# The output projection of a hybrid decoder block as seven Strassen products

## The chip, the cores and the metric

The kernel runs on one core of a Trainium2 chip. Its time is the device time in microseconds of one execution, as the median of three runs; the profile is of one further execution. Engines are named as the profile names them: PE is TensorE's matmuls, PEld its weight loads, DVE VectorE, ACT ScalarE, POOL GpSimd, SP SyncE, which only issues transfers here.

## The reference

One decoder block on 512 tokens of 1024 features in float32. Two mixers, retention and windowed attention, are projected, gated and merged; the merged features go through the output projection `w_out` (1024 x 1024), a norm and a residual; then a squared-ReLU MLP of 4096 features.

```python
merged = jax.nn.sigmoid(gate_r) * y_r + jax.nn.sigmoid(gate_s) * y_s
x = x + rmsnorm(merged @ w_out[l], post_mix_norm[l])
h = rmsnorm(x, pre_mlp_norm[l])
u = jnp.square(jax.nn.relu(h @ w_up[l]))
x = x + rmsnorm(u @ w_down[l], post_mlp_norm[l])
```

The change touches the second line, and how the third gets its input.

## The kernel before, in words

Every matmul on float32 data is done as three (`mm3`, L170 to L175): each operand is split into a rounded high part, which ScalarE writes (`split`, L129), and a low part, the rest, which VectorE writes (L130); then high x high, high x low and low x high are summed in a PSUM bank. So whatever is multiplied costs an instruction of ScalarE and one of VectorE first. `parts` does this for weights, into tiles `whi` and `wlo` of 128 x 1024 with four buffers each; `moving_parts` does it for a weight tile of 128 x 2048 in two halves. Raw weights arrive in `raw`, which has two buffers.

Most projections are already done in seven products of half-size blocks instead of eight (`wide` for the retention's values and its gate, `wino_pair` for the mixers' gates and the up projection). Sums of weight blocks that these need are partly made by transfers: a plain one brings a block (SP's queue), and one issued by POOL adds a second block onto it in SBUF.

The output projection is not among them. The merged features stand transposed in `sgr`, features on partitions, tokens along. The gates' last products end with sgr's last two blocks: `ret_proj` multiplies the retention's output (bank `yr`), VectorE scales it (L882) and adds the attention's part (L883). Each of the eight blocks is split into `mhi`, `mlo`. `w_out` comes in four pieces of 1 MB, split into `wo` (`load_wo`). Then, for tokens 0 to 255 and then 256 to 511, four banks `ps` take 24 matmuls of 512 columns each: 192 in all.

After each half follows the norm chain, marked to go ahead of other work (CHAIN_AHEAD): ScalarE squares each bank with a running sum (L951), VectorE weighs it with the gain (L976) and forms the mean (L952, L121), POOL takes the reciprocal root (`rstd`, L122), VectorE adds the residual into `x1` (L977), ScalarE squares that (L951), and after the same few steps VectorE writes h2 (L981, into `zg`). TensorE transposes h2 (L1029, bank `tin`, 16 of 128 x 128 for each half of the tokens), ScalarE and VectorE split it into `h2c` for the first half and `h2b`, `h2d` for the second, and the first three pairs of up blocks (`first_ups`, bank `up`, 24 matmuls of 256 columns each) run on it while the sums for the Strassen part of the up projection are made (`wino_tokens`).

The tile framework orders each engine's instructions from the program's order and the given priorities; within an engine they start in that order.

Of the kernel before, what the change touches and what calls it, by code (L numbers as in the profile page):

```python
# [10 lines left out]
F32 = mybir.dt.float32  # L11
F32R = mybir.dt.float32r
# [4 lines left out]
P = 128  # L17
D_MODEL = 1024
SEQ = 512
# [75 lines left out]
def block_kernel(ctx, tc, x, xT, pre_mix, w_in, w_v, w_g, w_gate, w_ret, w_swa, w_out, sinks, post_mix,  # L95
                 pre_mlp, w_up, w_down, post_mlp, decay, chunk, dist, out):
    nc = tc.nc
    x, out = x[0], out[0]
    w_in, w_ret, w_swa, w_out = (w[0] for w in (w_in, w_ret, w_swa, w_out))
# [6 lines left out]
    def bank(shape, name="ps"):  # L106
        return psum.tile(shape, F32, tag="ps", name=name)
# [19 lines left out]
    def split(hi, lo, src):  # L127

        last["hi"] = nc.scalar.copy(hi, src)  # L129
        last["split"] = nc.vector.tensor_tensor(lo, src, f(hi), op=ALU.subtract)  # L130

    def raw_tile(shape):
        return stream.tile(shape, F32, name="raw", tag="raw", bufs=2)
# [30 lines left out]
    def moving_parts(raw):  # L164
        nr, width = raw.shape[1], raw.shape[2]
        h = nr // 2
        tiles = [parts(raw[:, i * h : (i + 1) * h, :], [P, h, width]) for i in range(2)]
        return [(tiles[k // h][0][:, k % h, :], tiles[k // h][1][:, k % h, :]) for k in range(nr)]

    def mm3(ps, a, b, first, last, more=False):  # L170

        (ah, al), (bh, bl) = a, b
        nc.tensor.matmul(ps, ah, bh, start=first, stop=False, skip_group_check=more)  # L173
        nc.tensor.matmul(ps, ah, bl, start=False, stop=False, skip_group_check=more)  # L174
        nc.tensor.matmul(ps, al, bh, start=False, stop=last, skip_group_check=more)  # L175

# [695 lines left out]
    def ret_proj(bp, wr):  # L872

        for b in range(2):
            fb = 2 * bp + b
            ps = bank([P, SEQ], "yr")
            for k in range(KD):
                mm3(
                    ps, tuple(a[:, k, :] for a in wr[b]),
                    tuple(a[:, k, :] for a in retT), k == 0, k == KD - 1,  # L880
                )
            nc.vector.tensor_tensor(sig[fb], ps, sig[fb], op=ALU.mult)  # L882
            nc.vector.tensor_add(sig[fb], sig[fb], ys[fb])  # L883
# [11 lines left out]
    hctx.close()  # L895


    wctx = ExitStack()
    wpool = wctx.enter_context(tc.tile_pool(name="wpool", bufs=1))
    mctx = ExitStack()  # L900
    mpool = mctx.enter_context(tc.tile_pool(name="mpool", bufs=16))
    fctx = ExitStack()
    wo = []

    def load_wo(n, pool):
        wo.append([pool.tile([P, KD, 512], F32R, name=f"wo{i}{n}") for i in range(2)])
        for kq in range(2):
            raw = raw_tile([P, 4, 512])
            nc.sync.dma_start(
                raw,  # L910
                w_out[kq * 512 : (kq + 1) * 512, n * 512 : (n + 1) * 512].rearrange(
                    "(k p) c -> p k c", p=P
                ),
            )
            for k2 in range(2):
                sl = slice(kq * 4 + k2 * 2, kq * 4 + k2 * 2 + 2)
                split(wo[n][0][:, sl, :], wo[n][1][:, sl, :], raw[:, k2 * 2 : k2 * 2 + 2, :])

    merged = []
    for bp in range(KD // 2):  # L920
        if bp == KD // 2 - 1:
            ret_proj(bp, wr)
            load_wo(0, wpool)
        for b in range(2):
            hi = mpool.tile([P, SEQ], F32R, name="mhi", tag="m")
            lo = mpool.tile([P, SEQ], F32R, name="mlo", tag="m")
            split(hi, lo, sig[2 * bp + b])
            merged.append((hi, lo))
# [8 lines left out]
    tmp = tctx.enter_context(tc.tile_pool(name="tmp", bufs=3, side="right"))  # L937
    fpool = fctx.enter_context(tc.tile_pool(name="fpool", bufs=1))
    load_wo(1, fpool)
# [3 lines left out]
    nc.sync.dma_start(g_mlp, pre_mlp.to_broadcast([P, D_MODEL]))  # L943
    for t in range(NT):
        nc.sync.dma_start(x1[t], x[t * P : (t + 1) * P, :])

    def square_sum(srcs, junk):
        ss = small.tile([P, 2], F32, name="ss2")
        for i, s in enumerate(srcs):
            c = slice(i * 512, (i + 1) * 512)  # L950
            nc.scalar.activation(junk[:, c], s, AF.Square, accum_out=ss[:, i : i + 1])  # L951
        nc.vector.tensor_add(ss[:, 0:1], ss[:, 0:1], ss[:, 1:2])  # L952
        return rstd_of(ss[:, 0:1], 1, 1.0 / D_MODEL)

    h2 = []
    for half in range(2):
        zs = [[None, None], [None, None]]
        for n in range(2):
            for t in range(2):
                tt = 2 * half + t  # L960
                ps = bank([P, 512])
                for k in range(KD):
                    mm3(
                        ps, tuple(a[:, tt * P : (tt + 1) * P] for a in merged[k]),
                        tuple(a[:, k, :] for a in wo[n]), k == 0, k == KD - 1,
                    )
                zs[t][n] = ps
        with tc.high_priority(offset=CHAIN_AHEAD):
            for t in range(2):
                tt = 2 * half + t  # L970
                hn = tmp.tile([P, D_MODEL], F32, name="zg")
                r = square_sum(zs[t], hn)
                zg = tmp.tile([P, D_MODEL], F32, name="zg")
                for n in range(2):
                    c = slice(n * 512, (n + 1) * 512)
                    nc.vector.tensor_tensor(zg[:, c], zs[t][n], g_post[:, c], op=ALU.mult)  # L976
                nc.vector.scalar_tensor_tensor(  # L977
                    x1[tt], zg, r[:, 0:1], x1[tt], op0=ALU.mult, op1=ALU.add
                )
                r = square_sum([x1[tt][:, :512], x1[tt][:, 512:]], hn)  # L980
                nc.vector.scalar_tensor_tensor(hn, x1[tt], r[:, 0:1], g_mlp, op0=ALU.mult, op1=ALU.mult)  # L981
                h2.append(hn)

    NH = 3
    fctx.close()
    mctx.close()
    wctx.close()
# [355 lines left out]
```

## Time and profile before

| | |
|---|---|
| three runs | 730.77, 731.11, 731.98 us; median 731.11 |
| the profiled execution | 731.96 us |
| its span | 730.2 us |
| granted TensorE clock, mean | 0.997 |
| PE busy | 718.1 us, 98% of the span |
| DVE, ACT, POOL busy | 535.6, 423.8, 60.5 us |
| output projection, first matmul | at 356.2 us of the span |
| first transposes of h2 | at 394.55 us |
| second transposes of h2 | at 410.27 us |

A row of a window gives its length, then for each engine the busy time and the number of instructions, then the granted clock, the mean busy share of the transfer engines and their rate. A row of the timeline gives start, duration, engine, line, operation, what is written and read; in brackets the idle time before it and what ended that. Successive instructions overlap in the records: what one costs its engine is the distance between starts, not the duration.

### The profile page before, as it was taken

What the parts mean: (1) busy time and instruction counts of PE and PEld (TensorE: products, weight loads), DVE (VectorE), ACT (ScalarE), POOL (GpSimd) and SP (SyncE); (2) the same over time, 40 slices, a digit from 0 to 9 for tenths busy, and PEclk for the clock granted to TensorE, in tenths of its full rate; (3) what the DMA queues carried; (4) which work ended last, traced back from release to release, by engine and by line L of the source; (5) the groups of instructions that cost most, each with busy time, mean ns of one, the idle gap of its engine ahead of it and who ended that gap; (6) DMA issues with size and microseconds to landing.
All of it is one profiled execution on the core that took longest, in us unless ns stands there. A gap on an engine that the chain in (4) does not pass through costs nothing.

```text
span 730.2 us, 11250 instructions
## 1 busy us (share of the span) xinstructions
PE 718.1 (98%) x4438; PEld 640.3 (88%) x4438; DVE 535.6 (73%) x808; ACT 423.8 (58%) x714; POOL 60.5 (8%) x75
## 2 busy tenths in 40 slices
PE   8999999999999999999999999999999999999996
PEld 8877878888888999989888999999999888888885
DVE  5699976677975756566944866677676788987797
ACT  6667676445665534435634865766667756555571
POOL 0200000211100000000011101100000010010010
PEclk9999999999999999999999999999999999999998
DMA  9954434907444446543661619766753899698603
GB/s 314 331 170 85 104 83 144 289 4 145 87 144 117 143 117 179 151 133 115 216 247 58 160 49 283 198 172 169 197 147 117 266 291 238 156 203 200 116 0 116
DMA packets 43749, 117.79 MB, mean 161 GB/s; under 512 B 3504, under 2 KB 21296, under 8 KB 37552
## 3 DMA queue, kind: packets, MB, share of 16 engines
q1 hardware_dynamic: 36928, 80.76, 31.5%
q0 software_dynamic: 6480, 36.18, 26.4%
q8 instruction: 35, 0.57, 0.3%
q10 hardware_dynamic: 288, 0.14, 0.1%
q14 instruction: 18, 0.15, 0.1%
HBM read 114.96 MB, written 2.10 MB: 160 GB/s over the span
## 4 chain that ended last, share of the span: by engine, by line
PE 67%; DVE 5%; DMA 2%; issue 1%; ACT 1%; POOL 1%; POOLq 0%; DVEq 0%; ACTq 0%
PE wino L173 10%; PE wino L174 10%; PE wino L175 10%; PE p L174 5%; PE p L173 5%; PE p L175 5%; PE yr L173 2%; PE yr L174 2%; PE ps L174 2%; PE yr L175 2%; PE ps L175 2%; PE ps L173 2%; DVE wlo L130 2%; PE up L175 2%; PE up L174 2%; PE up L173 2%
## 5 line engine op out<-in xcount | busy, mean ns | idle before, releaser
L130 DVE TENSOR_TENSOR wlo<-raw,whi 128x1024 fp32r<-128x1024 f32 x81 | 98.6, 1222 | 49.6 <-ACT whi L129 49.6
L129 ACT CAST whi<-raw 128x1024 fp32r<-128x1024 f32 x81 | 84.7, 1051 | 41.4 <-DMA raw<-in_w_down 7.5
L174 PE MATMUL p<-wlo,left 128*128 128x512 f32 x216 | 84.2, 390 | 0.0
L175 PE MATMUL p<-whi,left 128*128 128x512 f32 x216 | 84.1, 390 | 0.0
L173 PE MATMUL p<-whi,left 128*128 128x512 f32 x216 | 84.0, 390 | 0.1
L175 PEld LDWEIGHTS p<-whi,left 128*128 128x128 f32 x216 | 40.5, 188 | 9.1 <-DVE left L130 0.8
L174 PEld LDWEIGHTS p<-wlo,left 128*128 128x128 f32 x216 | 40.6, 188 | 8.7 <-DVE wlo L130 0.3
L173 PEld LDWEIGHTS p<-whi,left 128*128 128x128 f32 x216 | 40.5, 188 | 8.8 <-ACT left L129 0.5
L130 DVE TENSOR_TENSOR wlo<-tch,whi 128x1024 fp32r<-128x1024 f32 x32 | 38.6, 1219 | 7.5 <-ACT whi L129 7.5
L129 ACT CAST left<-uc 128x1024 fp32r<-128x1024 f32 x28 | 29.3, 1052 | 23.2 <-PE p L174 23.2
L130 DVE TENSOR_TENSOR left<-uc,left 128x1024 fp32r<-128x1024 f32 x28 | 34.1, 1220 | 10.2 <-ACT left L129 10.2
L129 ACT CAST p<-rs 128x1024 fp32r<-128x1024 f32 x21 | 22.0, 1050 | 31.2 <-DVE rs L224 31.2
L129 ACT CAST whi<-tch 128x1024 fp32r<-128x1024 f32 x32 | 33.2, 1050 | 11.7 <-PE p L175 6.8
L130 DVE TENSOR_TENSOR p<-rs,p 128x1024 fp32r<-128x1024 f32 x21 | 25.7, 1225 | 14.7 <-ACT p L129 14.7
L130 DVE TENSOR_TENSOR wlo<-rs,whi 128x1024 fp32r<-128x1024 f32 x21 | 25.7, 1224 | 10.5 <-ACT whi L129 8.4
L173 PE MATMUL wino<-h2c,whi 128*128 128x256 f32 x104 | 29.4, 283 | 0.0
L174 PE MATMUL wino<-h2c,whi 128*128 128x256 f32 x104 | 29.4, 283 | 0.0
L175 PE MATMUL wino<-h2c,wlo 128*128 128x256 f32 x104 | 29.4, 283 | 0.0
L174 PE MATMUL wino<-h2s,p 128*128 128x256 f32 x104 | 29.4, 283 | 0.0
L175 PE MATMUL wino<-h2s,p 128*128 128x256 f32 x104 | 29.4, 283 | 0.0
L173 PE MATMUL wino<-h2s,whi 128*128 128x256 f32 x104 | 29.4, 283 | 0.0
L174 PE MATMUL wino<-h2s,whi 128*128 128x256 f32 x104 | 29.4, 283 | 0.0
(350 smaller groups left out, 2328.7 us busy)
## 6 DMA issues: line engine op xcount, KB each, us to landing
tch<-in_w_down POOLq DMA_DIRECT2D x12, 1024.0 KB, 9.6
raw<-in_w_down SPq DMA_DIRECT2D x7, 1024.0 KB, 7.6
rs<-in_w_up SPq DMA_DIRECT2D x13, 512.0 KB, 4.1
rs<-in_w_up POOLq DMA_DIRECT2D x13, 512.0 KB, 5.4
raw<-in_w_up SPq DMA_DIRECT2D x13, 512.0 KB, 5.1
raw<-in_w_in SPq DMA_DIRECT2D x8, 512.0 KB, 5.3
acc<-in_w_v POOLq DMA_DIRECT2D x4, 1024.0 KB, 8.0
rs<-in_w_gate SPq DMA_DIRECT2D x8, 512.0 KB, 3.7
```

What stands on the lines that cost most here:

```text
L129: last["hi"] = nc.scalar.copy(hi, src)
L130: last["split"] = nc.vector.tensor_tensor(lo, src, f(hi), op=ALU.subtract)
L173: nc.tensor.matmul(ps, ah, bh, start=first, stop=False, skip_group_check=more)
L174: nc.tensor.matmul(ps, ah, bl, start=False, stop=False, skip_group_check=more)
L175: nc.tensor.matmul(ps, al, bh, start=False, stop=last, skip_group_check=more)
```

## The change

With the four blocks of the merged features (token half, feature half) m11, m12, m21, m22 and the four blocks of the weights, the projection becomes seven products of 24 matmuls each, into two banks for the two blocks of 128 tokens. `w_out` is laid out beforehand in blocks of 512 x 512, so that one plain transfer brings a block. The sums of weight blocks `ta` and `tb2` are made by one plain and one or two adding transfers; `b22` is used once as it came, then block (1,0) is added onto it by a transfer and it is used again; `tb2` is used once, then VectorE adds `b21` onto it (L1048 of the changed file) and it is used again. The sums of the merged features are made in place by VectorE (L952, L1024, L1025, L1036). Results leave the banks through copies on ScalarE and sums on VectorE into SBUF (L1021, L1043, L1055), and for tokens 0 to 255 the squares and the weighing (L994) read them there. The norm chain then runs for two blocks of tokens at once (L1000 the residual, L1010 h2). The first transposes of h2 are told to stand behind the last matmul of the products. The shared scratch for `zg` gets a fourth buffer. The core of the diff:

```diff
+    tb2 = weight_sum("tb2")
+    n22, n11, a12 = merge_parts("n22"), merge_parts("n11"), merge_parts("a12")
+    ta = weight_sum("ta")
+    b22 = weight_sum("b22")
+    s1, s4, s2 = (merge_parts(n) for n in ("s1", "s4", "s2"))
+    copies = [opool.tile([P, 2, 512], F32, name=f"copy{i}") for i in range(3)]
...
+    def t_load(dst, *blocks):
+        for n, (i, j) in enumerate(blocks):
+            if n:
+                nc.gpsimd.dma_start(dst, w_out[i, j], accum_op=ALU.add)
+            else:
+                nc.sync.dma_start(dst, w_out[i, j])
...
+    w11 = moving_parts(wide_load(w_out, 0, 0))
+    b21 = wide_load(w_out, 0, 1)
+    t_load(ta, (0, 0), (1, 0))
+    t_load(b22, (1, 1))
+    t_load(tb2, (0, 0), (1, 0), (1, 1))
+    split_scaled(n11[0], n11[1], m11, -1.0)
+    ret_proj(KD // 2 - 1, wr)
+    split(a12[0], a12[1], m12)
+    w21 = moving_parts(b21)
+    nc.vector.tensor_tensor(m21, m21, m22, op=ALU.subtract)
+    split(s1[0], s1[1], m21)
...
+    product(chain, n11, w11)
+    for tb in range(2):
+        nc.scalar.copy(copies[0][:, tb], chain[tb])
+    product(p2, a12, w21)
+    for tb in range(2):
+        nc.vector.tensor_tensor(zcols(tb, 0), p2[tb], copies[0][:, tb], op=ALU.subtract)
+        weighed(tb, 0)
+    nc.vector.tensor_tensor(m11, m11, m21, op=ALU.subtract)
+    nc.vector.tensor_tensor(m12, m12, m11, op=ALU.subtract)
+    product(p35, s1, moving_parts(ta))
+    split(s4[0], s4[1], m12)
...
+    w = moving_parts(b22)
+    nc.gpsimd.dma_start(b22, w_out[1, 0], accum_op=ALU.add)
+    product(p35, s4, w, False)
+    split(s2[0], s2[1], m11)
+    split_scaled(n22[0], n22[1], m22, -1.0)
+    nc.vector.tensor_tensor(m22, m22, m11, op=ALU.subtract)
...
+        w = moving_parts(tb2)
+    product(chain, s2, w, False)
+    with tc.high_priority(offset=CHAIN_AHEAD):
+        for tb in range(2):
+            nc.scalar.copy(copies[2][:, tb], chain[tb])
+            ins = nc.vector.tensor_tensor(zcols(tb, 1), p35[tb], copies[2][:, tb], op=ALU.add)
+            weighed(tb, 1)
...
+        nc.vector.tensor_tensor(tb2, tb2, b21, op=ALU.add)
+    s3 = merge_parts("s3", "n11")
+    split(s3[0], s3[1], m22)
+    product(chain, s3, moving_parts(b22), False)
+    with tc.high_priority(offset=CHAIN_AHEAD):
+        for tb in range(2):
+            z = copies[1][:, tb]
+            nc.vector.tensor_tensor(z, chain[tb], z, op=ALU.add)
+        normed((0, 1))
...
+    product(chain, n22, moving_parts(tb2), False)
+    with tc.high_priority(offset=CHAIN_AHEAD):
...
+        normed((2, 3))
...
-    with tc.high_priority(offset=H2_AHEAD):
+    with tc.issue_after(last["mm"].ins), tc.high_priority(offset=H2_AHEAD):
         transpose_h2(0)
```

In the order of instructions three places show what moves. First VectorE from the last block of the merged features on. Before (`mlo`: low halves of the merged features, `wo`: of w_out):

```order
L882 TENSOR_TENSOR sgr_2343<-yr_3577,sgr_2343 128x512
L130 TENSOR_TENSOR wo11_3644<-raw_3645,wo01_3643 128x1024
L883 TENSOR_TENSOR sgr_2343<-sgr_2343,ys_2150 128x512
L130 TENSOR_TENSOR wo11_3644<-raw_3645,wo01_3643 128x1024
L130 TENSOR_TENSOR mlo_3623<-sgr_2343,mhi_3622 128x512
L130 TENSOR_TENSOR wo11_3644<-raw_3651,wo01_3643 128x1024 x2
L976 TENSOR_TENSOR zg_3774<-ps_3665,g_post_3657 128x512
```

And now (`wlo_3622` is a half of w21, `wlo_3721` and `wlo_3725` are those of `ta`, `a12` and `s1` low halves of operands):

```order
L882 TENSOR_TENSOR sgr_2343<-yr_3588,sgr_2343 128x512
L883 TENSOR_TENSOR sgr_2343<-sgr_2343,ys_2150 128x512
L130 TENSOR_TENSOR wlo_3622<-raw_3551,whi_3621 128x1024
L952 TENSOR_TENSOR sgr_2343<-sgr_2343 128x4x256
L130 TENSOR_TENSOR a121_3529<-sgr_2343,a120_3528 128x1024
L1024 TENSOR_TENSOR sgr_2343<-sgr_2343 128x4x256
L130 TENSOR_TENSOR s11_3533<-sgr_2343,s10_3532 128x1024
L1025 TENSOR_TENSOR sgr_2343<-sgr_2343 128x4x256
L1021 TENSOR_TENSOR zg_3704<-p2_3652,copy0_3538 128x512
L130 TENSOR_TENSOR wlo_3721<-ta_3530,whi_3720 128x1024
L994 TENSOR_TENSOR zg_3704<-zg_3704,g_post_3642 128x512
L130 TENSOR_TENSOR wlo_3725<-ta_3530,whi_3724 128x1024
```

Where four splits and then the norm stood, there now stand sums and splits of operands and of weight sums, the first results between them.

Second, VectorE ahead of h2 of the first tokens. Before, with `wlo` halves of the up weights:

```order
L952 TENSOR_TENSOR ss2_3766<-ss2_3766 128x1
L976 TENSOR_TENSOR zg_3774<-ps_3715,g_post_3657 128x512
L121 TENSOR_SCALAR ms_3770<-ss2_3766 128x1
L977 SCALAR_TENSOR_TENSOR x1_3632<-zg_3774,rstd_3771,x1_3632 128x1024
L130 TENSOR_TENSOR wlo_4022<-raw_4019,whi_4021 128x1024
L130 TENSOR_TENSOR wlo_4026<-raw_4019,whi_4025 128x1024
L952 TENSOR_TENSOR ss2_3778<-ss2_3778 128x1
L976 TENSOR_TENSOR zg_3796<-ps_3690,g_post_3657 128x512
```

And now, from the second use of `b22` on (`wlo_3842`, `wlo_3846`; `wlo_3918` is of `tb2` after its last sum):

```order
L130 TENSOR_TENSOR s31_3838<-sgr_2343,s30_3837 128x1024
L130 TENSOR_TENSOR wlo_3842<-b22_3531,whi_3841 128x1024
L130 TENSOR_TENSOR wlo_3846<-b22_3531,whi_3845 128x1024
L1043 TENSOR_TENSOR zg_3704<-p35_3718,copy2_3540 128x512
L1048 TENSOR_TENSOR tb2_3523<-tb2_3523,raw_3551 128x2048
L994 TENSOR_TENSOR zg_3704<-zg_3704,g_post_3642 128x512
L1043 TENSOR_TENSOR zg_3710<-p35_3719,copy2_3540 128x512
L988 TENSOR_TENSOR ss2_3706<-ss2_3706 128x1
L130 TENSOR_TENSOR wlo_3918<-tb2_3523,whi_3917 128x1024
L1055 TENSOR_TENSOR copy1_3539<-chain_3650,copy1_3539 128x512
L994 TENSOR_TENSOR zg_3710<-zg_3710,g_post_3642 128x512
L121 TENSOR_SCALAR ms_3876<-ss2_3706 128x1
```

The norm of the first tokens now stands behind and between the weight halves of the last two products, whose sources are sums.

Third, TensorE at the first transposes of h2. Before:

```order
L174 MATMUL ps_3859<-wo11_3644,mhi_3622 128x512
L175 MATMUL ps_3859<-wo01_3643,mlo_3623 128x512
L173 MATMUL ps_3884<-wo01_3643,mhi_3526 128x512
L1029 MATMUL tin_3987<-ident_67,zg_3765 128x128
L1029 MATMUL tin_3987<-ident_67,zg_3787 128x128
```

And now:

```order
L173 MATMUL chain_3651<-whi_3921,n220_3524 128x512
L174 MATMUL chain_3651<-wlo_3922,n220_3524 128x512
L175 MATMUL chain_3651<-whi_3921,n221_3525 128x512
L1113 MATMUL tin_4019<-ident_67,zg_3886 128x128
L1113 MATMUL tin_4027<-ident_67,zg_3886 128x128
L1113 MATMUL tin_4035<-ident_67,zg_3886 128x128
L1113 MATMUL tin_4043<-ident_67,zg_3886 128x128
L1113 MATMUL tin_4019<-ident_67,zg_3896 128x128
```

They stood at the start of the last bank's 24 matmuls, with 23 behind them; now all 168 are ahead of them, and four need only the first 128 tokens' h2. The second sixteen stand behind 73 up matmuls before, behind 61 (four of them) and 67 (twelve) now. On POOL the adding transfers of `ta`, `tb2` (two) and `b22` stand ahead of the first reciprocal root.

More of the change, by code (lines that the diff above doesn't have):

```diff
@@ L174, in mm3 @@
         nc.tensor.matmul(ps, ah, bl, start=False, stop=False, skip_group_check=more)
-        nc.tensor.matmul(ps, al, bh, start=False, stop=last, skip_group_check=more)
+        return nc.tensor.matmul(ps, al, bh, start=False, stop=last, skip_group_check=more)
     def wino_pool(stack, side="left"):
@@ L919, in block_kernel, with weight_sum @@
[L919 to L928, printed above, removed]
+    octx = ExitStack()
+    opool = octx.enter_context(tc.tile_pool(name="opool", bufs=1))
+    def weight_sum(name):
+        return opool.tile([P, 4, 512], F32, name=name)
@@ new lines, in block_kernel, with merged, product @@
+    ta = weight_sum("ta")
+    b22 = weight_sum("b22")
+    s1, s4, s2 = (merge_parts(n) for n in ("s1", "s4", "s2"))
+    copies = [opool.tile([P, 2, 512], F32, name=f"copy{i}") for i in range(3)]
+    def merged(i, j):
+        return sgr[:, 2 * j : 2 * j + 2].rearrange("p m (b h) c -> p m b h c", h=2)[:, :, :, i]
+    m11, m12, m21, m22 = (merged(i, j) for i in range(2) for j in range(2))
+    def product(ps, a, w, first=True):
+        for tb in range(2):
+            for k in range(4):
+                last["mm"] = mm3(
+                    ps[tb], tuple(o[:, k // 2, k % 2, tb * P : (tb + 1) * P] for o in a), w[k],
+                    first and k == 0, k == 3, not first,
+                )
@@ L929, in block_kernel, with two @@
+    def two(name):
+        return [bank([P, 512], name) for _ in range(2)]
+    w11 = moving_parts(wide_load(w_out, 0, 0))
[9 more added lines that the diff above has]
+    split(s1[0], s1[1], m21)
     actx.close()
@@ L942, in block_kernel @@
     nc.sync.dma_start(g_post, post_mix.to_broadcast([P, D_MODEL]))
-    nc.sync.dma_start(g_mlp, pre_mlp.to_broadcast([P, D_MODEL]))
     for t in range(NT):
         nc.sync.dma_start(x1[t], x[t * P : (t + 1) * P, :])
[L947 to L951, printed above, removed]
+    nc.sync.dma_start(g_mlp, pre_mlp.to_broadcast([P, D_MODEL]))
@@ L952, in square_sum, with sum_rstd @@
+    def sum_rstd(ss):
         nc.vector.tensor_add(ss[:, 0:1], ss[:, 0:1], ss[:, 1:2])
         return rstd_of(ss[:, 0:1], 1, 1.0 / D_MODEL)
[L955 to L982, printed above, removed]
@@ new lines, in block_kernel @@
+    with tc.issue_after(after.ins):
+        nc.vector.tensor_tensor(tb2, tb2, b21, op=ALU.add)
[3 more added lines that the diff above has]
+    with tc.high_priority(offset=CHAIN_AHEAD):
+        for tb in range(2):
+            z = copies[1][:, tb]
+            nc.vector.tensor_tensor(z, chain[tb], z, op=ALU.add)
+        normed((0, 1))
+        for tb in range(2):
+            z = copies[1][:, tb]
+            c = part(2 + tb, 1, z)
+            nc.vector.tensor_tensor(zcols(2 + tb, 1), z, g_post[:, c], op=ALU.mult)
```

83 lines of the change are left out of this document (57 added, 26 removed).

## The prediction

> **What bounds the kernel now.** I read the page's shares and chain first, then the stage around the output projection in windows.
>
> ```profile
> PE 718.1 (98%) x4438; PEld 640.3 (88%) x4438; DVE 535.6 (73%) x808; ACT 423.8 (58%) x714; POOL 60.5 (8%) x75
> PE 67%; DVE 5%; DMA 2%; issue 1%; ACT 1%; POOL 1%; POOLq 0%; DVEq 0%; ACTq 0%
> core 0: us, PE busy (x) PEld busy (x) DVE busy (x) ACT busy (x) POOL busy (x), PEclk, DMA share, GB/s
> 345.00:356.20 11.20, 11.20 (x53) 9.34 (x52) 10.53 (x14) 8.62 (x14) 0.00 (x0) 1.00 0.47 158
> 356.20:367.00 10.80, 10.80 (x49) 8.93 (x48) 7.89 (x10) 5.21 (x7) 0.00 (x0) 1.00 0.92 338
> 367.00:378.00 11.00, 11.00 (x51) 9.09 (x50) 3.84 (x6) 4.21 (x9) 0.57 (x1) 1.00 0.58 241
> 378.00:389.00 11.00, 11.00 (x50) 9.13 (x49) 7.94 (x14) 4.64 (x12) 3.56 (x3) 1.00 0.52 192
> 389.00:402.00 13.00, 13.00 (x70) 11.06 (x69) 6.06 (x12) 6.13 (x16) 0.55 (x1) 1.00 0.00 1
> 402.00:413.00 11.00, 10.98 (x94) 10.77 (x93) 9.03 (x14) 8.47 (x20) 3.42 (x5) 1.00 0.81 192
> ...
> 424.00:438.00 14.00, 14.00 (x119) 14.00 (x118) 7.06 (x7) 9.04 (x16) 0.00 (x0) 1.00 0.20 63
> ```
>
> TensorE fills every window: from 356.2 (call it T0, the first output-projection matmul) on, this stage is bound by TensorE alone. VectorE is busy 7.89 + 3.84 + 7.94 + 6.06 = 25.7 of 45.8 us up to 402: it has some 20 us to spare there, no more.
>
> ```profile
> 356.20:394.30 38.10, 38.07 (x168) 31.53 (x168) 2.73 (x4) 3.38 (x10) 1.00 0.58 221
> 394.55 1.91 PE L1029 MATMUL tin<-ident,zg 128*128 128x128 f32 x16
> 401.40:410.30 8.90, 8.78 (x73) 8.79 (x73) 0.75 (x2) 1.00 0.68 176
> 410.27 2.13 PE L1029 MATMUL tin<-ident,zg 128*128 128x128 f32 x16
> 412.15 0.36 PE L174 MATMUL up<-h2c,whi 128*128 128x256 f32 x1
> ```
>
> The first row is of the projection's bank alone, the third of the up projection's: 168 matmuls of 512 columns take 38.1 us (0.227 each), 73 of 256 columns 8.75 (0.12). Transposes stand between, unwaited for; the second sixteen are over at 412.15 = T0 + 55.95, with 73 up matmuls done.
>
> **TensorE's part.** Seven products of 24 matmuls replace 192: 168, over at T0 + 38.1 if nothing is late. 24 x 0.227 = 5.45 us go. But all 16 first transposes now stand behind the 168, where they had 23 projection matmuls behind them as cover. They need h2 of tokens 0 to 255, so the question is when VectorE has it.
>
> **VectorE's part.** Counted by form, it gets 17 more instructions of 1024 elements (splits of seven weight sums and seven operand sums, the sums themselves), one of 2048, and two fewer of 512. Their prices:
>
> ```profile
> 349.31 1.22 DVE L130 TENSOR_TENSOR wo<-raw,wo 128x1024 fp32r<-128x1024 f32 x1
> 350.44 0.68 DVE L130 TENSOR_TENSOR mlo<-sgr,mhi 128x512 fp32r<-128x512 f32 x1
> 351.04 0.69 DVE L882 TENSOR_TENSOR sgr<-yr,sgr 128x512 f32<-128x512 f32 x1
> 344.14 0.69 DVE L281 TENSOR_TENSOR sgs<-sgs,wino 128x512 f32<-128x512 f32 x1 [1.46 <-PE wino L175]
> 402.61 1.29 DVE L981 SCALAR_TENSOR_TENSOR zg<-x,rstd,g_mlp 128x1024 f32<-128x1024 f32 x1 [0.73 <-POOL rstd L122]
> 403.81 0.15 DVE L952 TENSOR_TENSOR ss<-ss 128x1 f32<-128x1 f32 x1
> 408.24 0.15 DVE L121 TENSOR_SCALAR ms<-ss 128x1 f32<-128x1 f32 x1
> 408.54 0.56 POOL L122 TENSOR_TENSOR rstd<-ms,mhalf 128x1 f32<-128x1 f32 x1 [0.65 <-DVE ms L121]
> 409.14 1.28 DVE L981 SCALAR_TENSOR_TENSOR zg<-x,rstd,g_mlp 128x1024 f32<-128x1024 f32 x1 [0.74 <-POOL rstd L122]
> ```
>
> From start to start: 1.14 for 1024 elements, 0.60 for 512 (from PSUM too; rows of 256 as in L281 cost no more), 1.20 for the norm's 1024, some 0.1 for the smallest. The one of 2048 has no row: 2.2 (two of 1024) to 2.4 (two durations); I take 2.2, since starts, not ends, follow each other. Net 17 x 1.14 + 2.2 - 1.2 = 20.4 us: what was spare is gone. So I walk its queue from T0 in the new order, where the last mixer block's product (L882) is ready at 0.2.
>
> (a) To the low half of `b22`, 17 rows: 2 x 0.6 and 0.1 for their dependence, six of 1.14 (one weight half, three sums, two operand splits), then 4 x 0.6 and 5 x 1.14: ends at 16.5. Every input is there by then: the second product's first bank, for L1021, at 5.45 + 2.7 = 8.2 against 8.4.
>
> (b) Only now may the transfer that adds block (1,0) onto `b22` start.
>
> ```profile
> acc<-in_w_g POOLq DMA_DIRECT2D x4, 1024.0 KB, 8.0
> 171.76 8.02 DMA acc<-in_w_g
> 179.80 1.06 ACT whi L129
> 180.88 1.23 DVE L130 TENSOR_TENSOR wlo<-acc,whi 128x1024 fp32r<-128x1024 f32 x1 [2.27 <-ACT whi L129]
> tch<-in_w_down POOLq DMA_DIRECT2D x12, 1024.0 KB, 9.6
> DMA to landing us min/median/max: 6.1/8.0/12.7
> raw<-in_w_out SPq DMA_DIRECT2D x4, 1024.0 KB, 5.1
> ```
>
> The retention's gate does the same thing already: an adding transfer of 1 MB lands 8.0 us after its issue, ScalarE rounds, VectorE subtracts. Nothing else is moving at T0 + 17 (the 2.5 MB of x and gains, which lie in 356.2 to 367, are through), so I take 8.0, not the 9.6 of the crowded stage nor the 6.1 that the shortest of `acc`, plain ones included, shows: issue 16.6, landing 24.6, ScalarE's cast to 25.7. VectorE, with six more rows of 1.14, is free at 23.3 and waits 2.4. ScalarE's queue stands behind that cast too: the copies and squares of tokens 0 to 255 follow it.
>
> (c) From 25.8: two low halves (28.1), then in VectorE's order eight of 0.6, 2.2 for `tb2`, three weight halves, three norm operations of 1.20 and 0.8 of small ones = 4.8 + 2.2 + 3.4 + 3.6 + 0.8 = 14.8. h2 of the first 128 tokens is there at **42.9**, of the next at **44.1**. TensorE meets this twice: the seventh product, due at 32.7, needs the low halves of `tb2`, which by the same walk begin at 32.2 and 34.7, so it stands some 1.5 us and ends near 39.7; then it stands 3.1 us until 42.9, does four transposes, stands until 44.1, does twelve (1.25 us).
>
> (d) The second half: 1.4 (two products with the gain, small sums), four low halves of h2 with small ones 2.6, two norm operations 2.4, three low halves of up weights 3.4 and 0.3 small: 54.2; two norm operations: 55.4 and 56.6; twelve transposes: **57.95**, with 67 up matmuls done. The second pair's weights wait in this queue as well, so up matmuls stand some 2.5 us for them.
>
> Against before: 57.95 - 55.95 = 2.0 us later, and 73 - 67 = 6 matmuls of 0.12 still owed: **+2.7 us**. The rest is equal: up matmuls and, behind them, the next stage; VectorE makes up its lag while they run (it was idle 7 of the 14 us after 424).
>
> The other transfers I cost at nothing. `ta` and `tb2` can load only when the last gate product has read hsum, 12 matmuls of 0.12 after L281's 344.14, near 345.6; plain megabytes landed in 5.1, so `ta`'s sum is complete near T0 + 2 (used at 5) and `tb2`'s two additions, 8 each, near 16 (used at 17.5, and ScalarE has 2 us to spare behind it). POOL issues `b22`'s after them, in turn. If that cover goes, it is (b) again, us for us. The reciprocal root on POOL stood 0.15 + 0.56 behind VectorE and is hidden in (c) by the rows between.
>
> **The clock.** TensorE stands 3.1 us at one place, as nowhere since the start.
>
> ```profile
> 1.37 3.36 PE L330 MATMUL warm<-ident 128*128 128x128 f32 x14 [1.37 <-POOL ident masks.py:199]
> 722.74 0.28 PE L175 MATMUL p4c<-whi,left 128*128 128x256 f32 x1
> 725.00:726.00 1.00, 0.00 (x0) 0.00 (x0) 0.50 (x1) 0.00 (x0) 0.47 (x1) 0.74 0.00 0
> 726.00:728.00 2.00, 0.00 (x0) 0.00 (x0) 1.05 (x3) 0.00 (x0) 0.00 (x0) 0.50 0.44 159
> ```
>
> After the last matmul the granted clock fell to half within 2.5 us, so here it should fall too. At the start 14 pieces took 0.24 each, twice the 0.12 of the sixteen transposes. If half speed lasts 3.4 us (about the warm-up's length) from the first transposes, it covers those and a few up matmuls, most of which would wait for VectorE anyway: +0.3. If it lasts through the first 24 up matmuls (2.9 us more), ScalarE's first Relu comes that much later, and the squares of tokens 256 to 511 stand behind it; less a slack of 1 us: +1.9. Below zero it can't go. I take 0.3. The Trainium skill, "TensorE: Matmul & The Clock Gate" (Part 1), says half rate follows an idle window of about 3.4 us and ends after a busy one of as much, the windows running freely; by that a wait of 3.1 holds none, and the sum would be +2.7. The trace's end, with 2.5 us, speaks for a shorter wait being enough, and I follow it.
>
> Sum: +3.0. The profiled execution took 731.96 around its span of 730.2, 0.85 above the median of 731.11; 731.96 + 3.0 = 735.0, as a median **734.1**.
>
> **Rivals.** (1) *The clock stays half through the first up block*: +2.7 + 1.9 = 4.6, so 735.7. For it the fall at 725; against it that the first up matmuls stand close. (2) *The addition onto `b22` lands early*: at 22.2, when ScalarE comes free of the last operand split. VectorE then begins (c) at 23.4 instead of 25.8: +2.7 - 2.4 = +0.3, 731.4, no measurable change. Against it the 8.02 above. The Trainium skill, "DMA: Bandwidth & Descriptors" ("Anatomy of one DMA — SWDGE (gpsimd) path"), fits 2.0 us + bytes / 436e3, an estimate of 4.4 us for 1 MB; by it the sum would be this rival's; the adding transfers of this trace take nearly twice that. (3) *The saving stays*: TensorE never stands, 731.1 - 5.45 = 725.7. h2 would have to be there at 38.1, 4.8 us before my walk; rival 2 gives 2.4 of it, the rest would need VectorE's rows some 5% shorter than any row shows. It decides once the walk to h2 ends before T0 + 40 or so.
>
> **Numbers.** Forecast 0.63, (1) 0.17, (2) 0.13, (3) 0.07. A change under 0.2% (1.5 us) can't be told from none here: slower 0.80, same 0.13, faster 0.07. The forecast's own range is 732.8 to 735.0: VectorE's starts 2% either way over 57 us. The whole range goes from rival 2 (731.3) to rival 1 with the transfer at 9.6 instead of 8.0 (735.7 + 1.6 = 737.3).
>
> **What would show it.** TensorE idle about 1.5 us in the seventh product and 3 before the first transposes of h2, both released by VectorE; 2 to 3 us more before up matmuls; VectorE nearly full from 357 to 410 but for one wait of about 2.4 for the second use of `b22`, ended by an adding transfer of 8 us; a granted clock under 1 near 400. I am wrong if the transposes follow the 168 at once, or if a weight sum is late in the first four products.

## The result, and the profile after

The changed kernel takes 742.27 us (median of four runs, 741.82 to 743.03) against 731.30 for the kernel before (four runs, 730.77 to 731.98): ratio 1.0148, 95% interval 1.0136 to 1.0160. It is slower by 11.0 us, where 3.0 was forecast; 742.27 lies above the whole range that the prediction gave (731.3 to 737.3). The profiled execution took 743.03 around a span of 741.2. The page's shares and chain:

```profile
PE 721.0 (97%) x4414; PEld 642.5 (87%) x4414; DVE 554.7 (75%) x824; ACT 435.4 (59%) x725; POOL 65.1 (9%) x79
PE 37%; DVE 4%; issue 1%; DMA 1%; ACT 1%; POOL 0%; POOLq 0%; DVEq 0%; ACTq 0%
```

The shares hardly differ from those of before; the loss sits in one stage. Its windows, with the columns and bounds of the prediction's table:

```profile
356.20:367.00 10.80, 10.80 (x49) 8.93 (x49) 9.98 (x10) 7.33 (x9) 0.87 (x1) 1.00 1.02 261
367.00:378.00 11.00, 7.76 (x23) 5.85 (x22) 7.76 (x9) 5.34 (x9) 1.58 (x2) 0.69 1.04 330
378.00:389.00 11.00, 10.63 (x47) 8.44 (x46) 7.01 (x7) 6.09 (x7) 0.18 (x1) 1.00 0.68 141
389.00:402.00 13.00, 12.87 (x56) 9.86 (x54) 12.54 (x17) 9.13 (x21) 3.09 (x2) 1.00 0.24 81
402.00:413.00 11.00, 7.10 (x46) 6.56 (x46) 10.23 (x21) 8.17 (x19) 4.37 (x6) 0.84 0.51 139
413.00:424.00 11.00, 9.37 (x67) 9.38 (x68) 9.59 (x14) 6.96 (x19) 1.99 (x2) 0.84 0.75 244
```

TensorE is no longer full: 23 matmuls where there were 51 (367 to 378), 46 where there were 94 (402 to 413). In the first two windows the transfer engines are full (share 1.02 and 1.04, before 0.92 and 0.58). VectorE is idle for 3.2 and 4.0 us in the second and third, where the walk had one wait of 2.4. The waits view of VectorE from 357 to 406, in us in total, times, longest:

```profile
DVE wlo L130 <- ACT whi L129: 3.9, 1, 3.9
DVE zg L994 <- DMA g_post<-in_post_mix_norm: 3.8, 1, 3.8
DVE sgr L882 <- PE yr L175: 2.9, 1, 2.9
DVE x L1000 <- POOL rstd L122: 0.5, 1, 0.5
DVE zg L1010 <- POOL rstd L122: 0.4, 1, 0.4
```

The third row lies before the first product. The first is `tb2`: ScalarE rounds it only when its sum has come. The transfers, from issue to landing (last column), the adding ones on POOL's queue:

```profile
tb<-in_w_out POOLq DMA_DIRECT2D x2, 1024.0 KB, 12.2
ta<-in_w_out SPq DMA_DIRECT2D x1, 1024.0 KB, 5.0
ta<-in_w_out POOLq DMA_DIRECT2D x1, 1024.0 KB, 12.8
b<-in_w_out POOLq DMA_DIRECT2D x1, 1024.0 KB, 9.1
g_post<-in_post_mix_norm SPq DMA_DIRECT2D x1, 512.0 KB, 13.7
```

Each addition was forecast at 8.0, and the gain `g_post`, 6.3 before, was not in the sum at all. What TensorE meets, with two rows of VectorE and one of POOL:

```profile
372.12 0.79 PE L174 MATMUL p<-wlo,s 128*128 128x512 f32 x1 [3.24 <-DVE wlo L130]
405.68 3.62 PE L1113 MATMUL tin<-ident,zg 128*128 128x128 f32 x16 [3.81 <-ACT whi L129]
390.51 2.28 DVE L1048 TENSOR_TENSOR tb<-tb,raw 128x2048 f32<-128x2048 f32 x1
392.71 0.68 DVE L994 TENSOR_TENSOR zg<-zg,g_post 128x512 f32<-128x512 f32 x1
396.55 1.55 POOL L122 TENSOR_TENSOR rstd<-ms,mhalf 128x1 f32<-128x1 f32 x1 [18.37 <-DVE ss L988]
```

The first transposes start at 405.68, 49.4 us behind the first product (T0 = 356.25); the walk said 42.9. The profile names a cast of ScalarE as what ended TensorE's wait. But h2 is what sets it: in each of the fourteen kernels that were run with the change the first transposes start 1.43 or 1.44 us behind the start of VectorE's first row of h2 (404.25 here), whatever is named. The row of 2048 elements takes 2.20 from start to start, as assumed. POOL's root takes 1.55, not the 0.56 of the prediction's row. In the kernel before it had both lengths already: 1.55 and 1.46 (at 383.02) beside VectorE rows with two inputs in SBUF, 0.55 to 0.57 where VectorE stood or its row read a bank:

```profile
379.35 1.55 POOL L122 TENSOR_TENSOR rstd<-ms,mhalf 128x1 f32<-128x1 f32 x1 [4.40 <-DVE ms L121]
```

### The profile page after: what moved, and what is told of

Its sections match the earlier page's. It is cut to its first block, busy times and chain, and to the rows that moved or that the text cites. A ratio compares the mean times of both kernels' runs of the same rounds, so it can differ in the third digit from the quotient of the medians.

```text
span 741.2 us, 11260 instructions
## 1 busy us (share of the span) xinstructions
PE 721.0 (97%) x4414; PEld 642.5 (87%) x4414; DVE 554.7 (75%) x824; ACT 435.4 (59%) x725; POOL 65.1 (9%) x79
## 5 line engine op out<-in xcount | busy, mean ns | idle before, releaser
L130 DVE TENSOR_TENSOR wlo<-raw,whi 128x1024 fp32r<-128x1024 f32 x85 | 103.5, 1222 | 49.9 <-ACT whi L129 49.7
L129 ACT CAST whi<-raw 128x1024 fp32r<-128x1024 f32 x85 | 89.1, 1052 | 45.2 <-PE yr L174 8.1
L175 PEld LDWEIGHTS p<-whi,left 128*128 128x128 f32 x216 | 40.5, 188 | 9.1 <-DVE left L130 0.8
L174 PEld LDWEIGHTS p<-wlo,left 128*128 128x128 f32 x216 | 40.5, 188 | 8.9 <-DVE wlo L130 0.4
L173 PEld LDWEIGHTS p<-whi,left 128*128 128x128 f32 x216 | 40.5, 188 | 8.7 <-ACT left L129 0.5
```

What stands on the lines that cost most here:

```text
L175: return nc.tensor.matmul(ps, al, bh, start=False, stop=last, skip_group_check=more)
```

## The experiments

Three theories. **A**: VectorE's queue sets h2, every wait in it moves h2 by as much, and the unforecast waits come from transfers that crowd each other. **B**: VectorE's longer queue alone. **C**: the halved TensorE clock. All edits are to the changed kernel.

**e1, `tb2` summed by VectorE.**

```diff
-    t_load(tb2, (0, 0), (1, 0), (1, 1))
...
+    nc.vector.tensor_tensor(tb2, ta, b22, op=ALU.add)
     nc.gpsimd.dma_start(b22, w_out[1, 0], accum_op=ALU.add)
```

> VectorE makes the sum of tb2 from ta and b22 (one row of 128x2048, 2.2 us) and tb2's three transfers, 3 MB, are gone. Theory A (the adding transfers crowd the queues: g_post's gain comes 14 us after its issue, tb2's sum lands at 381.8, and the walk of VectorE's queue gives the rest): g_post and ta land 4 to 6 us earlier, the third product runs without its wait of 3.6 us, the fifth product is no more held until 384; 735 to 738. Theory B (VectorE's longer queue alone is the loss): 2.2 us more of VectorE ahead of h2, so 744.5. Theory C (the half clock after the wait in the third product is most of the loss): as A if that wait goes, with clock 1.0 from 371 to 378.

Measured 746.25 (ratio 1.0199, interval 1.0184 to 1.0214): slower than the changed kernel, a miss for A, and slower than B's number too. VectorE's timeline shows why:

```profile
360.93 2.29 DVE L1031 TENSOR_TENSOR tb<-ta,b 128x2048 f32<-128x2048 f32 x1 [8.18 <-DMA ta<-in_w_out]
```

The sum was put first in VectorE's queue, which then stood until `ta`'s addition landed at 360.9, with the last mixer block's product queued behind it. The edit made a wait of its own: it doesn't settle the matter.

**e2, `tb2` summed by GpSimd.** The sum takes the place of the three transfers, on POOL.

```diff
-    t_load(tb2, (0, 0), (1, 0), (1, 1))
+    nc.gpsimd.tensor_tensor(tb2, ta, b22, op=ALU.add)
```

> The same sum of tb2 from ta and b22, made by GpSimd instead of VectorE; tb2's three transfers are gone. A: as with the sum on VectorE but 2 us less of VectorE's queue, if GpSimd needs under 10 us for 128x2048: 734 to 736. B: VectorE's rows are the same as in the changed kernel, so 742. C: as A.

Measured 742.18 (1.0143, 1.0128 to 1.0158): B's number again. Its timeline, one row of POOL and two of VectorE:

```profile
360.77 5.13 POOL L947 TENSOR_TENSOR tb<-ta,b 128x2048 f32<-128x2048 f32 x1 [9.93 <-DMA ta<-in_w_out]
361.33 5.66 DVE L130 TENSOR_TENSOR s<-sgr,s 128x1024 fp32r<-128x1024 f32 x1
366.91 1.21 DVE L1025 TENSOR_TENSOR sgr<-sgr 128x1024 f32<-128x1024 f32 x1
```

A VectorE row of 1.14 took 5.58 from start to start: it began beside POOL's addition and was over about 1 us behind the end of that. The waits for `g_post` and `tb2` are gone. In their place came 4.44 us of standing inside an instruction, which no waits view lists, and a wait of 2.85 for `b22`'s addition. The Trainium skill, "SBUF — State Buffer" ("Who interferes with whom"), says that a VectorE instruction with two SBUF inputs contends with a GpSimd one that reads SBUF, and that this contention is an exclusive lock; this row agrees.

**e4, `g_post` first.** It is loaded ahead of the stage's weights.

```diff
+    g_post = opool.tile([P, D_MODEL], F32, name="g_post")
+    nc.sync.dma_start(g_post, post_mix.to_broadcast([P, D_MODEL]))
...
-        junk = opool.tile([P, 512], F32, name="junk")
+        junk = copies[0][:, t % 2]
```

To make room, the squares' unused output goes into `copies[0]`; e3 and e10 have the same.

> Only the gain g_post is loaded earlier, ahead of the weights of this stage; all adding transfers stay. A: the wait of 3.8 us at the weighing and the half clock from 371 to 378 go, but tb2's second addition still lands near 382, and the fifth product waits for that: 741 to 742.5, no gain to speak of. B: 742. C: the half clock of 6.8 us and the wait of 3.6 us in the third product go, so 736 to 738.

Measured 742.54 (1.0149, 1.0129 to 1.0170), as A and B said. The wait at the weighing only shrank, from 3.77 to 2.51: VectorE waits for ScalarE's squares, which stand behind casts that stood 2.57 us for `ta`'s sum. (The moved output is not what did it: e5 below, without the move, has a wait of 2.72 at the same place.) The wait for `tb2`'s sum grew from 3.94 to 5.12. The half clock behind the first wait shrank from 6.8 to 3.4 us without any gain, so C is hit but not yet ruled out.

**e3, x and the second gain behind `tb2`'s sum.** As e4, with these loads held back by a tiny copy out of `tb2`.

```diff
+    for t in range(NT):
+        nc.gpsimd.tensor_copy(x1[t][:, :1], tb2[:, 0, :1])
...
+    for t in range(NT):
+        nc.sync.dma_start(x1[t], x[t * P : (t + 1) * P, :])
```

> The gain g_post early, and the 2.5 MB of x and the second gain held back until tb2's sum has landed, so that the adding transfers run with fewer plain loads beside them. A: tb2's additions take 8 to 9 us each instead of 13.3 and 11.1, its sum is there near 374 to 376, no wait in the third product; 734 to 737. B: 742. C: 736 to 738, as with g_post early alone.

Measured 748.15 (1.0224, 1.0207 to 1.0241), a miss for all. The additions:

```profile
tb<-in_w_out POOLq DMA_DIRECT2D x2, 1024.0 KB, 9.3
b<-in_w_out POOLq DMA_DIRECT2D x1, 1024.0 KB, 12.7
```

`tb2`'s second addition, now without x beside it, took 7.97 instead of 11.08; `b22`'s, with x moved onto it, 12.71 instead of 9.14, and VectorE waited 9.06 for it. It was also issued late, at 379.99 instead of 377.31, behind the tiny copies in POOL's queue. The crowding had been moved to the addition with the least room.

**e5, e6, e7: additions left out one after the other.** `tb2`'s two; then `ta`'s as well; then `b22`'s.

```diff
-    t_load(tb2, (0, 0), (1, 0), (1, 1))
+    t_load(tb2, (0, 0))
...
-    t_load(ta, (0, 0), (1, 0))
+    t_load(ta, (0, 0))
...
-    nc.gpsimd.dma_start(b22, w_out[1, 0], accum_op=ALU.add)
```

> The two additions onto tb2 are left out (tb2 is one plain block, so the output is not the reference's); nothing takes their place on any engine. Theory A (VectorE's queue sets h2, and every wait in it moves h2 by as much; in the changed kernel it waits 3.8 for g_post and 3.9 for tb2, both late because the adding transfers crowd the queues): both waits go, a wait of 2.8 for the second use of b22 comes, so 742.3 - 4.9 = 737.4, between 736.5 and 738. Theory B (VectorE's rows alone, whatever the transfers do): 742. Theory C (the half clock is most of the loss): 736 or less if the clock stays full, and the gain goes with the clock, not with the waits.

> As the run with tb2 plain, and the addition onto ta left out too; b22's addition stays. A: ta's sum was in time with tb2's additions gone, so nothing more is won than there: 737, between 736 and 738. B: 742. C: as with tb2 plain.

> All four adding transfers of this stage left out, b22 used twice as it came. A: the wait of 2.8 for b22's second use goes too, 734.5, between 733.5 and 735.5; what is left over the kernel before is VectorE's rows alone. B: 742. C: as with tb2 plain, about 736.

Measured 740.39 (1.0121, 1.0103 to 1.0140), 737.35 (1.0082, 1.0066 to 1.0098) and 734.29 (1.0040, 1.0024 to 1.0056). VectorE's rows are the same in number and kind, and 8.0 us go with the additions: B falls. C asked for 736 or less on e5 if the clock stays full; it does from the first product until 0.4 us before the first transposes, and 740.39 speaks against C for that stretch. A's numbers came on e6 and e7, and A was 3 us too low on e5. On e6 the number is right and its reason isn't: "`ta`'s sum was in time" in e5 is what failed there, and e6 gained the 3 us that it was to leave alone. The waits views of VectorE of e5, without the rows of POOL and `yr`, and of e7, whole:

```profile
DVE wlo L130 <- ACT whi L129: 3.4, 1, 3.4
DVE zg L994 <- ACT junk L979: 2.7, 1, 2.7
```

```profile
DVE sgr L882 <- PE yr L175: 2.9, 1, 2.9
DVE x L1000 <- POOL rstd L122: 0.5, 1, 0.5
DVE zg L1010 <- POOL rstd L122: 0.4, 1, 0.4
```

In e5 `ta`'s addition still took 12.7: in e2 it had taken 10.7, with the plain loads of `b22` and the up weights in SP's queue, and here `tb2`'s stands there too. ScalarE stood 2.85 for `ta`, and the squares that VectorE waits for stood behind its cast. In e6 the addition onto `b22` is the only one, took 8.0, and cost a wait of 2.9.

**e8, the gap before the transposes filled.**

```diff
+    fill = bank([P, 512], "fill")
+    with tc.issue_after(last["mm"].ins):
+        for i in range(10):
+            last["mm"] = nc.tensor.matmul(
+                fill, n22[0][:, 0, 0, :P], n22[0][:, i % 2], start=i == 0, stop=i == 9
+            )
```

> The changed kernel with ten spare matmuls of 512 columns (2.3 us) between the last product and the first transposes of h2, where TensorE stands 4 us; every other engine's order is as in the changed kernel. C (the half clock after that gap costs): clock 1.0 from 405 to 409, 739.5 to 741. A (h2 sets it, the half clock lies beside VectorE's work): 741.5 to 742.8.

The window of the first transposes, of the changed kernel and of e8:

```profile
405.36:408.78 3.42, 3.00 (x13) 2.65 (x14) 3.03 (x7) 1.24 (x3) 0.20 (x1) 0.50 0.79 307
```

```profile
405.36:408.78 3.42, 2.93 (x24) 2.77 (x25) 3.39 (x10) 2.33 (x5) 1.29 (x3) 1.00 0.65 246
```

The clock stays full there, and the time is 741.60 (1.0139, 1.0123 to 1.0155), which can't be told from the changed kernel's. With e5, C falls as the main cause: this half clock lies beside VectorE's work, and the earlier one, from 371, was not there in e5 (nor in e7 and e10), whose transposes come by the same sum as those of the changed kernel (table below).

**e9, every weight sum ready.** e7 without VectorE's own addition onto `tb2`.

```diff
-    with tc.issue_after(after.ins):
-        nc.vector.tensor_tensor(tb2, tb2, b21, op=ALU.add)
```

> No adding transfers, and VectorE's addition onto tb2 (128x2048, 2.2 us, ahead of h2) left out too: what the products would take if every weight sum came ready by a plain load. Theory A (h2 comes 40.7 us after the first product plus every wait on VectorE, and the time follows h2): 734.3 - 2.2 = 732.1, between 731.3 and 733. Theory D (with the adding transfers gone something other than VectorE's queue bounds the stage): no gain, 734.3.

Measured 731.49 (ratio 0.9996, 0.9988 to 1.0005): level with the kernel before, as A said; D's number falls.

**e10 and e12, plain loads behind `b22`'s addition.** e12 moves x and the second gain and keeps every order on VectorE, ScalarE and TensorE; e10 also moves the first up weights there and `g_post` to the front.

```diff
-    for t in range(NT):
-        nc.sync.dma_start(x1[t], x[t * P : (t + 1) * P, :])
-    nc.sync.dma_start(g_mlp, pre_mlp.to_broadcast([P, D_MODEL]))
...
     nc.gpsimd.dma_start(b22, w_out[1, 0], accum_op=ALU.add)
+    late = [(x1[t], x[t * P : (t + 1) * P, :]) for t in range(NT)]
+    late += [(g_mlp, pre_mlp.to_broadcast([P, D_MODEL]))]
+    for d, src in late:
+        nc.gpsimd.tensor_copy(d[:, :1], b22[:, 0, :1])
+        nc.sync.dma_start(d, src)
```

> All transfers and VectorE's rows as in the changed kernel; only the plain loads not needed at once are moved: g_post ahead of the weights, and x, the second gain and the first up weights (3.5 MB) behind b22's addition. A: the adding transfers take near 8 us each instead of 9 to 13; ta in time or 1 late, tb2's sum at T0 + 21 (wait of 3), b22's at T0 + 27 (wait of 2): waits 5 to 6 instead of 7.7, 739.7, between 738 and 741. Rival (adding transfers are as slow by themselves, with no crowding): 742.

> The changed kernel with x and the second gain (2.5 MB) loaded behind b22's addition and nothing else moved: every instruction of VectorE, ScalarE and TensorE stands in the same order. A (plain loads beside the adding transfers make these long): tb2's additions take about 11 and 8.5 instead of 13.3 and 11.1, its sum is there near 377 and costs VectorE 0 to 1; ta still late by 2.7 as with tb2 plain (the up weights stay beside it), b22 by 2.5; waits 5.5 instead of 7.7 and g_post no longer among them: 739.8, between 738.8 and 741. Rival (the additions are as slow by themselves): 742.

e10 measured 742.45 (1.0142, 1.0123 to 1.0162), its profiled execution 739.56 and the other three 742.24 to 743.69. In the profile A's numbers hold up to the transposes (waits of 5.35, additions of 9.7, 9.2, 8.1, 8.1), but VectorE's and the up weights' order behind h2 changed too, and why the other runs are longer stays open. e12 measured 741.17 (1.0126, 1.0104 to 1.0148), 1 us under the changed kernel, not the 2.5 expected, and by the intervals not clearly under it. Its transfers, and what the view of tile `tb` gives for that buffer's three:

```profile
ta<-in_w_out POOLq DMA_DIRECT2D x1, 1024.0 KB, 12.5
b<-in_w_out POOLq DMA_DIRECT2D x1, 1024.0 KB, 8.2
g_post<-in_post_mix_norm SPq DMA_DIRECT2D x1, 512.0 KB, 13.8
DMA to landing us min/median/max: 7.9/10.8/12.5
```

The additions that ran without plain loads took 7.9 and 8.2 (the same two took 11.1 and 9.1 in the changed kernel): crowding is what made them long, the rival falls. The two that still ran beside the 1 MB of up weights, and in part beside each other, took 12.5 each, and so `g_post`, behind those weights in SP's queue, was as late as before. That it would come early was my mistake.

**f1, the sums made ahead in DRAM.** Four buffers are filled by four plain and seven adding transfers during the gates and loaded as plain blocks here.

```diff
+        for d in (d_ta, d_b22, d_tb2, d_tb2n):
+            nc.gpsimd.dma_start(d, w_out[1, 0], accum_op=ALU.add)
...
-    t_load(ta, (0, 0), (1, 0))
+    nc.sync.dma_start(ta, d_ta)
```

> The whole computation, with the four weight sums (b21's included) made by transfers between DRAM buffers some 90 us ahead and then loaded as plain blocks; no adding transfer and no VectorE addition on weights is left beside the products. A: as with the sums left out, 732.1, between 731 and 733.5, so level with the kernel before within 0.3%. Rival: the eleven DRAM transfers hold up the gates' weights in the stage before, and the gain is given back there: 735 or more, with the first product later than 357.

Measured 758.03 (1.0366, 1.0352 to 1.0380): the rival's case. The first product comes at 380.2, because the gates' weights were late, up to 37.6 us from issue to landing. One of the additions, and the longest wait of TensorE:

```profile
d_b<-in_w_out POOLq DMA_DIRECT2D x1, 1024.0 KB, 18.0
301.18 0.58 PE L173 MATMUL wino<-hT,whi 128*128 128x256 f32 x1 [7.93 <-ACT whi L129]
```

From the first product on, f1 takes 374.5 us; the kernel before takes 374.0. So even without that harm this way wins nothing.

**e11, VectorE relieved.** e9 without the four sums of the merged features.

```diff
-    nc.vector.tensor_tensor(m21, m21, m22, op=ALU.subtract)
-    nc.vector.tensor_tensor(m11, m11, m21, op=ALU.subtract)
-    nc.vector.tensor_tensor(m12, m12, m11, op=ALU.subtract)
-    nc.vector.tensor_tensor(m22, m22, m11, op=ALU.subtract)
```

> As the run with every weight sum ready, and the four sums of the merged features on VectorE (128x1024 each, 1.14 us from start to start, 4.6 us in all) left out as well. A (VectorE's queue is what ate the 24 matmuls): the first transposes follow the products at once, near T0 + 38.3 instead of 40.2, and 731.5 - 1.9 = 729.6, between 728.5 and 730.3, faster than the kernel before for the first time. D (the second half of the tokens and the up weights bound it by now): level, 731.5.

Measured 730.31 (0.9989, 0.9973 to 1.0005): by its ratio it can't be told from e9 (0.9996) nor from the kernel before. A has the transposes, D the time.

```profile
398.21 2.16 PE L1106 MATMUL tin<-ident,zg 128*128 128x128 f32 x12 [2.66 <-DVE zg L1009]
```

The first four transposes do follow the products, at T0 + 38.1; the next twelve wait 2.66 for h2 of the second 128 tokens. With 6.8 us of VectorE's rows taken out, the 24 matmuls saved still hardly show, and VectorE's queue is no longer the reason ahead of the transposes: it stands 6.97 us for ScalarE there, which itself stands for TensorE (four times in 371 to 382, 5.7 us). TensorE's own rows give the account: it has 5.45 us less to do, loses the 2.66, and then runs one window of 3.41 us (398.9 to 402.3) at half clock, an estimate of 1.7 us of work. That leaves 1.1, near the 0.8 of the ratio. In e9 it stands 1.96 and 1.39 us at the transposes and has a window of half clock too, which leaves an estimate of 0.4. So where TensorE itself sets the end, its stand and the half clock behind it do cost time; no run takes the half clock away there.

**All runs by one rule.** Waits are VectorE's between the first product and h2, added up from its timeline (in e2 with the 4.44 inside an instruction, in e1 with 5.3 by which its queue began late); rows are what an edit adds to VectorE's queue. e11 and f1 are not in it: in both VectorE's order changes, with two weighings of the second half (L1053 in e11, L1077 in f1) behind the first row of h2 instead of ahead of it, and the same sum would give 37.9 and 39.5.

| kernel | waits | rows | first transposes, from T0 | less waits and rows | median us |
|---|---|---|---|---|---|
| changed | 8.55 | 0 | 49.42 | 40.87 | 742.27 |
| e1 | 10.06 | +2.2 | 53.03 | 40.77 | 746.25 |
| e2 | 8.13 | 0 | 48.87 | 40.74 | 742.18 |
| e3 | 15.07 | 0 | 55.96 | 40.89 | 748.15 |
| e4 | 8.73 | 0 | 49.53 | 40.80 | 742.54 |
| e5 | 6.91 | 0 | 47.69 | 40.78 | 740.39 |
| e6 | 3.75 | 0 | 44.44 | 40.69 | 737.35 |
| e7 | 0.84 | 0 | 41.36 | 40.52 | 734.29 |
| e8 | 8.84 | 0 | 49.62 | 40.78 | 741.60 |
| e9 | 1.69 | -2.2 | 40.20 | 40.71 | 731.49 |
| e10 | 5.35 | 0 | 46.15 | 40.80 | 742.45 |
| e12 | 7.78 | 0 | 48.56 | 40.78 | 741.17 |

In these twelve the transposes come 40.5 to 40.9 us after the first product plus what VectorE stood; the walk without its wait gives 42.9 - 2.4 = 40.5. Waits and first transposes are of the profiled execution, which was the fastest of its four in e2 (741.38), e4 (741.03) and e10 (739.56). From the transposes to the end of the span these kernels take 333.3 to 336.8 us. The kernel before takes 335.7, with 23 matmuls of the projection still in it: the second half of the tokens takes back what these would save.

## Why the prediction was right on the sign and wrong on the size

Against a forecast of +3.0 stand +11.0 in the spans (741.2 - 730.2), by its steps:

- **TensorE's part** held as a sum. Its 168 matmuls would be over at T0 + 38.1; in e11 nothing holds them up and the transposes follow there. Its waits came elsewhere: 3.24 in the third product, 0.36 in the fifth and 3.81 before the transposes, where 1.5 in the seventh and 3.1 before the transposes were forecast.
- **VectorE's part, the walk itself,** held: 40.5 forecast, 40.5 to 40.9 in twelve kernels, the row of 2048 at 2.20.
- **"The other transfers I cost at nothing" failed**, and is most of the miss. `ta`'s sum was to be complete near T0 + 2 and came at T0 + 7.8 (364.08); `tb2`'s near T0 + 16 and came at T0 + 25.5 (381.78); x and the gains were to be "through" by T0 + 17, and the last landed at T0 + 25.4 (they are 3 MB, not the 2.5 that it says). That a weight sum is late in the first four products was a sign of being wrong by the prediction's own words, and `ta`'s was. I took 8.0 us for each addition and 5.1 for each plain megabyte, from rows of less crowded stages; here 4 MB of additions and 7 MB of plain loads shared the transfer engines within 41 us, at a share near 1 from 356 to 378. `g_post`, used at T0 + 10, had no term. So VectorE stood 3.77 and 3.94 instead of 2.4: **+5.3**. Leaving out the additions onto `tb2` and `ta` (e6) takes off 4.9 of the measured time, and without any addition (e7) 8.0 are gone.
- **(b)**, `b22`'s addition: in e6, where it alone is left, it is issued at T0 + 17.2 (forecast 16.6), takes 8.0 (8.0) and costs a wait of 2.9 (2.4). In the changed kernel VectorE came late for other reasons, and the 9.1 it took were hidden but for 0.2 us of ScalarE.
- **"The reciprocal root on POOL ... is hidden in (c)" failed**: the root takes 1.55 beside a working VectorE, and VectorE waits 0.46 and 0.38 for it: **+0.8**. I had priced it by a row of 0.56, at which VectorE stood; the rows of 1.55 and 1.46 at 379.35 and 383.02 of the same profile were there to read.
- **(c)** otherwise: 0.4 us late with the walk's own rows.
- **(d)**, the second half: 15.05 from the first transposes to the last was forecast, 16.6 measured: **+1.6**. VectorE waits 0.39 for ScalarE and 0.40 for POOL's root, which the walk had not. And from its second pair of h2 rows (417.50) to the transposes pass 2.43 us, in e7 1.43: up matmuls at half clock (415.60 to 419.02) stand ahead of them. That these cost the 1.0 is argued from the rows; no run takes them away alone. As forecast, 67 up matmuls were done by then; the 6 owed and what else lies behind are 0.9 of the loss.
- **The clock** was halved near 405, as said, and at 371 and 415.6, which was not. By e8 the one at the transposes costs nothing that can be measured in this kernel.

5.3 + 0.8 + 0.4 + 1.6 = 8.1 is the miss (the medians: 742.27 - 734.1 = 8.2). e7's 734.29, so near the forecast, is partly chance: it lacks the wait of 2.4 that I had counted and has about 2 of the small waits that I had not.

Rival 1's long half clock did not come: the clock was halved from 405.36 to 408.78, over the sixteen transposes alone, and the first up matmul (409.05) ran at full clock; rival 2 was wrong on the transfer, 7.9 or more in every run; rival 3's price is out of reach: e9 and e11, with more taken away than it asked for, stay level.

## What to carry to other kernels

When a change lengthens the queue of an engine until it sets the end, every transfer that this queue meets gets a price, us for us: list all of them with the moment of use, also those that the change doesn't touch (`g_post`), and give none at its lone duration while the transfer engines' share is near 1. Before moving work off such an engine, look for what the new place shares with it: GpSimd's addition of 5.13 us held up a VectorE row by 4.44, loads moved away from one addition slowed another, and sums made ahead held up the stage in which they were made. And work out the floor first: with every sum ready by itself (e9) the seven products only drew level, so no mending of the transfers could make this change pay.

## What the runs showed of the hardware

Additions by transfer lengthen each other's and the plain loads' way. Alone or nearly so, 1 MB took 7.9 to 8.2 in e1, e2, e3, e5, e6, e10 and e12; beside plain loads or each other 8.8 (in e8) to 13.3 (in the changed kernel) into SBUF and, in f1, up to 19.7 into DRAM, and the plain megabyte of up weights 17.0 beside them (4.7 alone). The Trainium skill, "DMA: Bandwidth & Descriptors" ("Queues, rings and completion order"), says that a transfer engine takes turns between the queues that have work for it; that both kinds slow here agrees.

The clock's changes lie multiples of 3.41 us apart in each run. Rows of windows of that length, PE busy in the first column behind the length; of e4, then of e5, then of the changed kernel, each with the window that follows:

```profile
367.54:370.95 3.41, 1.46 (x7) 0.90 (x6) 2.88 (x4) 2.74 (x5) 0.89 (x1) 1.00 0.99 368
370.95:374.37 3.42, 3.42 (x9) 2.67 (x8) 3.42 (x4) 0.95 (x3) 0.00 (x0) 0.50 1.08 414
```

```profile
368.74:372.15 3.41, 1.73 (x8) 1.42 (x9) 3.41 (x5) 2.64 (x5) 0.00 (x0) 1.00 0.22 87
372.15:375.57 3.42, 3.42 (x17) 2.83 (x16) 3.42 (x4) 1.26 (x3) 0.00 (x0) 1.00 0.00 0
```

```profile
412.19:415.60 3.41, 1.67 (x14) 1.47 (x14) 3.41 (x5) 2.91 (x10) 0.00 (x0) 1.00 1.07 210
415.60:419.02 3.42, 3.42 (x19) 3.42 (x18) 3.02 (x7) 0.29 (x2) 1.99 (x2) 0.50 0.95 356
```

A window with TensorE busy for 1.46 or 1.67 of its 3.41 us was followed by half clock, one with 1.73 was not. So a window need not be idle for it: a wait of 1.95 us (e4) was followed by half clock and one of 2.22 (e5) was not, by where they fall. But the busy time of a window doesn't settle it either. In e7 the window from 393.36, busy for 1.57, and in e3 the one from 407.60, busy for 1.44, were followed by full clock; what decides between such windows stays open. The Trainium skill, "TensorE: Matmul & The Clock Gate" (Part 1), has the freely running windows of this length; that only an idle one halves the clock, these rows don't bear out.
